# Moving the large SBUF tiles of a transformer layer by 32 bytes, on to multiples of 64 bytes

## The chip, the core and the metric

One core of a Trainium2 chip runs the whole layer as one program. The metric is device time in microseconds, the median of three runs. On this core TensorE (PE in the profile) multiplies, VectorE (DVE) and ScalarE (ACT) do the elementwise work, GpSimd (POOL) takes a few powers and sums, and the transfers are issued from SyncE (SP). SBUF, the memory on the core, has 128 partitions; a tile is a run of bytes at the same place of each partition, and "where a tile lies" below is that place, its address in the partition in bytes.

## What is computed

The layer has 512 rows of 1024 floats. Its parts, with the norms left out:

```
x = x + 0.5 * (silu(h @ wg) * (h @ wu)) @ wd          # ffn1, h = rmsnorm(x), hidden width 2816
h = rmsnorm(x)
o_a, o_b, o_c = three attentions on h @ w_in          # o_c attends to 256 memory rows
y = sum_i sigmoid(h @ w_gate_i + b_i) * (o_i @ w_branch_i)
x = x + y @ w_out
x = x + 0.5 * (silu(h @ wg) * (h @ wu)) @ wd          # ffn2
```

All of it is in float32.

## The kernel before

**Three matmuls for one.** A float32 operand is kept as a pair, hi and lo, of the faster type fp32r: `split` (lines 75 to 78) rounds it to hi on ACT (L77) and takes the difference lo on DVE (L78). A product then is three matmuls: hi by hi, hi by lo and lo by hi. In the profile's names of a matmul the first name behind the arrow is the **moving** operand, whose columns stream through the array, and the second is the **stationary** one, which a weight load (PEld) puts into the array before. Every matmul of the kernel has its own weight load, of 128 columns.

**The feed-forward layers.** `ffn` runs twice. The up product (`mm7`, L354) has as stationary operand a block of weights, 128 of whose columns are loaded at a time, and as moving operand 256 columns of M, the combined activations (`mhi`, `mlo`). Weight blocks go round a ring of six: four lie in the pool `base` (`whi`, `wlo`), two in the layer's own pool (`fhi`, `flo`). A job is 24 such matmuls to one PSUM bank. The down product (`mm3`, L110 to L112) has as stationary operand the gated hidden activations (`gh`, `gl`) and as moving operand 512 columns of a weight block, which again is `whi`/`wlo` or `fhi`/`flo` by turns of the same ring. So the same two kinds of weight tiles are met by M in the up product and by G in the down product.

**The mixing part.** Projections have 384 moving columns of a weight block (`whi`) against `hh`, `hl`, the rows of h, as stationary operand. Gates have 512 moving columns of `hh`, `hl` against weights `fh`, `fl`; branches have 512 moving columns of an attention's output (`och`, `oah`, `obh` and their lo halves) against `fh`, `fl`. The output product has a weight block against `yh`, `yl`. The order on TensorE in this part is written out by hand in the `PLAN_` strings; in the feed-forward layers `run_jobs` sets it.

**Where tiles lie.** Pools on the left side are stacked from the bottom of a partition up, those on the right side from the top down, and each tile takes a multiple of 32 bytes. `base` is first on the left and stays for the whole program; in it `mhalf` (L263, 32 bytes) comes after the identities, and later `le`, another small one. `hb` (96 bytes) lies in the pool `mix`. M and then h lie on the right side. In the built program of before this gives, as the remainder of the tile's address by 64 and by 128 (the offsets at which matmuls read inside them are all multiples of 128 bytes):

| tiles | before, by 64 | before, by 128 | changed, by 64 | changed, by 128 |
|---|---|---|---|---|
| `mhi`, `mlo` (M) | 32 | 96 | 0 | 64 |
| `whi`, `wlo` (base) | 32 | 32 | 0 | 64 |
| `fhi`, `flo` (ffn pool) | 0 | 64 | 0 | 0 |
| `gh`, `gl` (G) | 0 | 64 | 0 | 0 |
| `hh`, `hl` (h) | 32 | 96 | 0 | 64 |
| `fh`, `fl` (gate and branch weights) | 32 | 32 | 0 | 0 |
| `och`, `oah`, `obh`, `yh` and lo halves | 0 | 64 | 0 | 0 |
| `qk` | 0 | 64 | 0 | 0 |
| `kx` | 32 | 32 | 0 | 64 |
| `mkh`, `mkl` / `cqh`, `cql` | 32 / 32 | 32 / 32 | 0 / 0 | 64 / 0 |
| `wraw` (landing of weights) | 0 | 0 | 0 | 0 |

Of the kernel before, what the change touches and what calls it, by code (L numbers as in the profile page):

```python
# [11 lines left out]
F32 = mybir.dt.float32  # L12
# [6 lines left out]
P = 128  # L19
# [20 lines left out]

CHUNKS = (4, 6, 6, 6)
HS = S // 2
LAMBDA_INIT = 0.8 - 0.6 * math.exp(-0.3 * 0)
C_SCALE = 128 ** -0.5

# [2 lines left out]
def layer_kernel(ctx: ExitStack, tc: tile.TileContext, a: dict, out: bass.AP):  # L48
    nc = tc.nc

    base = ctx.enter_context(tc.tile_pool(name="base", bufs=1))
# [23 lines left out]
    def split(raw, hi, lo, engine=None):  # L75

        nc.scalar.copy(out=hi, in_=raw)  # L77
        (engine or nc.vector).tensor_tensor(out=lo, in0=raw, in1=f32(hi), op=ALU.subtract)  # L78
# [84 lines left out]
    def right_pool(name):  # L163
        return tc.tile_pool(name=name, bufs=1, side="right", reuse_waits="tile")
# [6 lines left out]
    def new_M(pool):  # L171
        mh, ml = (pool.tile([P, 7, 4, HS], F32R, name=n) for n in ("mhi", "mlo"))
        return {i: (mh[:, i - 1], ml[:, i - 1]) for i in range(1, 8)}
# [11 lines left out]
    class Operands:  # L185
# [19 lines left out]
        def combine(self, t):  # L205
# [17 lines left out]
            if t == 3:  # L223
                lo, hi = slice(0, HS), slice(HS, S)
                split(t1, *M[5])
# [7 lines left out]
    def squares(src):  # L233
# [4 lines left out]
            square_half(src[:, d], dump[:, d], ss[:, dh:dh + 1])  # L238
        return ss

    Mp = right_pool("M1")
    M1 = new_M(Mp.__enter__())
    memp = tc.tile_pool(name="memp", bufs=1, reuse_waits="tile")
# [15 lines left out]
    make_identity(nc, ident)  # L259
    identr = base.tile([P, P], F32R, name="identr")  # L260
    nc.vector.tensor_copy(out=identr, in_=ident)
    mhalf = base.tile([P, 8], F32, name="mhalf")
    nc.vector.memset(mhalf, -0.5)  # L263

    warm = bank("s")
# [66 lines left out]
    def ffn(pre, x_sb, M, fp, after, raws=None, before_last=None, after_half=None):  # L332
# [12 lines left out]
        def mm7(ps, blk, m, first):  # L345

            for j in range(2):
                c = slice(j * HS, (j + 1) * HS)
                for k in range(4):
# [7 lines left out]
        class Item:  # L357
# [47 lines left out]
            def gated(self, c, f, th):  # L405

                if self.pr[f] is None:
                    self.pr[f] = fp.tile([P, S], F32, tag="pr", name="pr", bufs=3)
                    self.n = 0
                sg = fp.tile([P, HS], F32, tag="sg", name="sg", bufs=2)  # L410
                nc.scalar.activation(out=sg, in_=c[:, :HS], func=AF.Silu)
                pr, cols = self.pr[f], slice(th * HS, (th + 1) * HS)
                nc.vector.tensor_tensor(out=pr[:, cols], in0=sg, in1=c[:, HS:], op=ALU.mult)
# [196 lines left out]
    for t in range(NT):  # L610
# [5 lines left out]
    nc.sync.dma_start(out=la, in_=a["a_lambda"].rearrange("(u v) d -> u v d", u=2).partition_broadcast(P))  # L616
    lp = heads(lam[:, 256:384], 2)
    nc.vector.tensor_tensor(out=lp, in0=la[:, :, 0, :], in1=la[:, :, 1, :], op=ALU.mult)
    le = base.tile([P, 4], F32, name="le")
    nc.vector.tensor_reduce(out=le[:, 0:2], in_=lp, axis=AX.X, op=ALU.add)  # L620
    nc.scalar.activation(out=le[:, 0:2], in_=le[:, 0:2], func=AF.Exp)
    nlam = le[:, 2:3]

    nc.vector.tensor_scalar(out=nlam, in0=le[:, 1:2], scalar1=-LAMBDA_INIT, scalar2=le[:, 0:1],
                            op0=ALU.add, op1=ALU.subtract)
# [13 lines left out]
    mp = mix.__enter__()  # L639


    def bcast(name, src, n):
        g = mp.tile([P, n], F32, name=name)
        nc.sync.dma_start(out=g, in_=src.partition_broadcast(P))
        return g

    gsub = bcast("gsub", a["a_sub_norm"], 128)
    nc.vector.tensor_scalar(out=gsub, in0=gsub, scalar1=1.0 - LAMBDA_INIT, scalar2=None, op0=ALU.mult)
    gb = mp.tile([P, 2, 64], F32, name="gb")
# [16 lines left out]
            nc.gpsimd.tensor_tensor(out=sg[:, :, c, o], in0=sg[:, :, c, o],  # L666
                                    in1=ga[:, c, i].unsqueeze(1).broadcast_to([P, NT, 32]), op=ALU.mult)

    hb = mp.tile([P, 24], F32, name="hb")
    with nc.allow_non_contiguous_dma(reason="3072 words, once"):  # L670
        nc.sync.dma_start(out=hb, in_=a["b_gate"].rearrange("(n p) -> p n", p=P))
    nc.vector.tensor_scalar(out=hb, in0=hb, scalar1=0.5, scalar2=None, op0=ALU.mult)
# [455 lines left out]
```

## Time and profile before

| | |
|---|---|
| median of three runs | 1274.46 us (1273.98 to 1274.72) |
| the profiled execution's own time | 1273.05 us |
| its span, first to last instruction | 1271.3 us |
| mean granted TensorE clock | 0.987 of full speed |
| PE busy / DVE busy / ACT busy | 97% / 66% / 47% of the span |

The span is what the trace shows; 1.75 us of the execution's time lie around it. A matmul's duration in the profile includes its way through the array, so matmuls that follow each other overlap, and the busy share of PE says that it always had one under way, not that it was at its peak. The distance from the start of a matmul to the start of the next is what counts for time.

### The profile page before, as it was taken

How to read it: one execution, taken by the hardware profiler on the slowest of the kernel's cores; microseconds unless marked ns; L12 is line 12 of the kernel's file. 1: busy time of each engine (PE TensorE's matmuls, PEld its weight loads, DVE VectorE, ACT ScalarE, POOL GpSimd, SP SyncE). 2: the span in 40 equal slices, each digit the busy share in tenths (PEclk: the TensorE clock that was granted, in tenths of full speed). 3: DMA queues.
4: the chain of work that ended last, by engine and by line, in shares of the span. 5: the costliest groups of instructions: out<-in, count | busy, mean ns of one | idle time of the engine just before them, and what ended most of it. 6: DMA issues, size and time to landing. Idle time of an engine off the chain costs nothing.

```text
span 1271.3 us, 19657 instructions
## 1 busy us (share of the span) xinstructions
PE 1232.4 (97%) x7808; PEld 1116.9 (88%) x7808; DVE 842.8 (66%) x1377; ACT 596.8 (47%) x1115; POOL 107.1 (8%) x108
## 2 busy tenths in 40 slices
PE   7799999999998999999999999999979999999997
PEld 7789989989986799999999999888878998998996
DVE  7977667667564756766765565453697766766753
ACT  7535425435443446554555454443463452543543
POOL 1100000000000301111221121020000000000002
PEclk8899999999999899999999999999989999999999
DMA  5533324322334403321222320254133242342311
GB/s 215 174 108 116 115 71 128 113 91 101 116 118 130 109 28 108 88 67 58 88 87 70 89 83 31 75 159 160 34 127 122 76 133 91 101 129 73 130 35 67
DMA packets 53084, 127.57 MB, mean 100 GB/s; under 512 B 10112, under 2 KB 10624, under 8 KB 52992
## 3 DMA queue, kind: packets, MB, share of 16 engines
q1 hardware_dynamic: 52416, 125.27, 30.9%
q8 instruction: 61, 1.00, 0.3%
q10 hardware_dynamic: 576, 1.05, 0.2%
q14 instruction: 31, 0.25, 0.1%
HBM read 122.11 MB, written 4.19 MB: 99 GB/s over the span
## 4 chain that ended last, share of the span: by engine, by line
PE 90%; DVE 4%; DMA 2%; ACT 1%; POOL 1%; issue 1%; SPq 0%; POOLq 0%; ACTq 0%; DVEq 0%
PE ps_s L354 19%; PE ps_g L110 9%; PE ps_g L112 9%; PE ps_g L111 9%; PE ps_o L354 5%; PE ps_p L110 4%; PE ps_p L354 4%; PE ps_p L111 4%; PE ps_p L112 4%; PE ps_g L354 4%; PE ps_s L110 2%; PE ps_s L112 2%; PE ps_s L111 2%; PE ps_o L881 2%; PE ps_s L849 2%; PE ps_t L697 1%
## 5 line engine op out<-in xcount | busy, mean ns | idle before, releaser
L77 ACT CAST whi<-wraw 128x1024 fp32r<-128x1024 f32 (+1 forms) x120 | 119.0, 993 | 141.3 <-PE ps_s L354 68.6
L78 DVE TENSOR_TENSOR wlo<-wraw,whi 128x1024 fp32r<-128x1024 f32 (+1 forms) x120 | 137.9, 1151 | 65.6 <-ACT whi L77 64.6
L354 PE MATMUL ps_s<-mhi,whi 128*128 128x256 f32 x496 | 138.3, 279 | 2.3 <-ACT snap L397 2.0
L354 PE MATMUL ps_s<-mlo,whi 128*128 128x256 f32 x496 | 137.7, 278 | 0.0
L354 PE MATMUL ps_s<-mhi,wlo 128*128 128x256 f32 x496 | 136.8, 278 | 0.0
L77 ACT CAST whi<-quarter 128x1024 fp32r<-128x1024 f32 x54 | 56.7, 1051 | 91.8 <-PE ps_s L354 22.7
L354 PEld LDWEIGHTS ps_s<-mhi,whi 128*128 128x128 f32 x496 | 93.8, 189 | 4.1 <-ACT snap L397 2.8
L110 PE MATMUL ps_p<-whi,hh 128*128 128x384 f32 (+1 forms) x264 | 94.8, 359 | 0.0
L354 PEld LDWEIGHTS ps_s<-mlo,whi 128*128 128x128 f32 x496 | 93.7, 189 | 1.0 <-DVE mlo L78 0.2
L354 PEld LDWEIGHTS ps_s<-mhi,wlo 128*128 128x128 f32 x496 | 93.2, 189 | 0.0
L112 PE MATMUL ps_p<-whi,hl 128*128 128x384 f32 (+1 forms) x264 | 89.2, 338 | 0.0
L111 PE MATMUL ps_p<-wlo,hh 128*128 128x384 f32 (+1 forms) x264 | 89.2, 338 | 0.0
L78 DVE TENSOR_TENSOR wlo<-quarter,whi 128x1024 fp32r<-128x1024 f32 x54 | 65.9, 1221 | 24.5 <-ACT whi L77 24.5
L110 PE MATMUL ps_g<-hh,fh 128*128 128x512 f32 x192 | 78.4, 408 | 0.0
L112 PE MATMUL ps_g<-hh,fl 128*128 128x512 f32 x192 | 75.8, 395 | 0.0
L111 PE MATMUL ps_g<-hl,fh 128*128 128x512 f32 x192 | 75.7, 394 | 0.0
L834 DVE CAST kx<-ps_t 128x256 fp32r<-128x256 f32 x32 | 13.6, 425 | 83.7 <-PE ps_t L832 83.7
L121 POOL TENSOR_TENSOR rsh<-msh,mhalf 128x4 f32<-128x4 f32 x38 | 45.2, 1191 | 276.9 <-DVE msh L127 225.2
L78 DVE TENSOR_TENSOR fl<-wraw,fh 128x768 fp32r<-128x768 f32 x48 | 50.0, 1042 | 26.1 <-ACT fh L77 26.1
L77 ACT CAST fhi<-quarter 128x1024 fp32r<-128x1024 f32 x34 | 35.5, 1049 | 59.1 <-PE ps_s L354 16.4
L354 PE MATMUL ps_s<-mhi,fhi 128*128 128x256 f32 x208 | 59.2, 285 | 2.5 <-ACT fhi L77 2.5
L354 PE MATMUL ps_s<-mlo,fhi 128*128 128x256 f32 x208 | 58.9, 283 | 0.0
(376 smaller groups left out, 3662.8 us busy)
## 6 DMA issues: line engine op xcount, KB each, us to landing
wraw<-in_ffn_w SPq DMA_DIRECT2D x88, 512.0 KB, 4.0
wraw<-in_ffn_wd SPq DMA_DIRECT2D x44, 512.0 KB, 3.9
wraw<-in_w_u SPq DMA_DIRECT2D x32, 384.0 KB, 3.3
wraw<-in_w_gb SPq DMA_DIRECT2D x32, 384.0 KB, 3.0
wraw<-in_w_gf SPq DMA_DIRECT2D x16, 384.0 KB, 3.1
wraw<-in_w_mem_kv SPq DMA_DIRECT2D x8, 512.0 KB, 4.1
wraw<-in_w_out SPq DMA_DIRECT2D x8, 512.0 KB, 4.5
x_sb<-in_x SPq DMA_DIRECT2D x4, 512.0 KB, 7.0
```

The costliest lines, as they stand in the source:

```text
L77: nc.scalar.copy(out=hi, in_=raw)
L78: (engine or nc.vector).tensor_tensor(out=lo, in0=raw, in1=f32(hi), op=ALU.subtract)
L110: nc.tensor.matmul(ps, lhsT=st[0], rhs=mv[0], start=first, stop=False)
L111: nc.tensor.matmul(ps, lhsT=st[0], rhs=mv[1], start=False, stop=False)
L112: return nc.tensor.matmul(ps, lhsT=st[1], rhs=mv[0], start=False, stop=last)
L121: nc.gpsimd.tensor_tensor(out=rs, in0=ms, in1=mhalf[:, :n], op=ALU.pow)
L354: nc.tensor.matmul(ps[:, c], lhsT=x, rhs=y, start=first and j + k + n == 0, stop=k == 3 and n == 2, skip_group_check=True)
L697: nc.tensor.transpose(ps[:, j * P:(j + 1) * P], pt[:, j * P:(j + 1) * P], ident)
L834: nc.vector.tensor_copy(out=un.kx[:, :, qs], in_=heads(p2[:, 0:256], 2))
L849: nc.tensor.matmul(out_, lhsT=q, rhs=k, start=j == 0, stop=j == 1)
L881: nc.tensor.matmul(o[:, vs], lhsT=pT[:, j * P:(j + 1) * P], rhs=un.v[:, j, vs], start=j == 0, stop=j == i)
```

## The change

Three small tiles are widened so that what lies behind them in their pool moves, and a pool of one 32-byte tile, which nothing reads or writes, is opened at the outer end of the right side before M.

```
+LINE = 16
...
+    linep = ctx.enter_context(tc.tile_pool(name="line", bufs=1, side="right"))
+    linep.tile([P, 8], F32, name="line")
     Mp = right_pool("M1")
...
-    mhalf = base.tile([P, 8], F32, name="mhalf")
+    mhalf = base.tile([P, LINE], F32, name="mhalf")
     nc.vector.memset(mhalf, -0.5)
...
-    le = base.tile([P, 4], F32, name="le")
+    le = base.tile([P, LINE], F32, name="le")
...
-    hb = mp.tile([P, 24], F32, name="hb")
+    hb = mp.tile([P, 2 * LINE], F32, name="hb")[:, :24]
```

On the left side, tiles behind `mhalf` move up by 32 bytes, those behind `le` by 64, those behind `hb` in its pool by 96; on the right side everything moves down by 32. Every large tile then lies on a multiple of 64 bytes (the table above). The instructions of all five engines and the transfers stand in the same order as before, with the same shapes and tiles; the one difference is that the memset of `mhalf`, once at the start on DVE, writes 128x16 elements instead of 128x8.

## Rows read from the trace of the kernel before

**Rows 1.** The page's part 1: busy us, share of the span, instructions.
```profile
PE 1232.4 (97%) x7808; PEld 1116.9 (88%) x7808; DVE 842.8 (66%) x1377; ACT 596.8 (47%) x1115; POOL 107.1 (8%) x108
```

**Rows 2.** Windows: each stretch's length, then busy us per engine, clock, DMA.
```profile
core 0: us, PE busy (x) PEld busy (x) DVE busy (x) ACT busy (x) POOL busy (x), PEclk, DMA share, GB/s
0.00:100.00 100.00, 84.50 (x545) 76.48 (x546) 82.07 (x102) 55.10 (x88) 11.01 (x12) 0.91 0.48 164
100.00:380.00 280.00, 280.00 (x1962) 259.64 (x1961) 193.52 (x234) 125.57 (x183) 2.20 (x4) 1.00 0.33 107
...
480.00:840.00 360.00, 359.76 (x2094) 325.46 (x2093) 221.82 (x581) 181.74 (x471) 63.97 (x60) 1.00 0.26 78
...
915.00:1000.00 85.00, 75.90 (x529) 70.22 (x528) 72.92 (x83) 41.98 (x56) 0.00 (x1) 0.96 0.34 112
1000.00:1200.00 200.00, 200.00 (x1443) 187.46 (x1442) 141.08 (x162) 87.83 (x121) 0.00 (x0) 1.00 0.31 99
```

**Rows 3.** Timeline of PE, first and last of a run: start us, duration us.
```profile
140.23 0.28 PE L354 MATMUL ps_s<-mhi,fhi 128*128 128x256 f32 x1
...
142.63 0.28 PE L354 MATMUL ps_s<-mhi,flo 128*128 128x256 f32 x1
142.75 0.28 PE L354 MATMUL ps_o<-mhi,whi 128*128 128x256 f32 x1
...
145.36 0.28 PE L354 MATMUL ps_o<-mhi,wlo 128*128 128x256 f32 x1
```

**Rows 4.** Groups by form, up product: count, busy us, mean ns, idle before.
```profile
L354 PE MATMUL ps_s<-mlo,whi 128*128 128x256 f32 x496 | 137.7, 278 | 0.0
...
L354 PE MATMUL ps_s<-mlo,fhi 128*128 128x256 f32 x208 | 58.9, 283 | 0.0
...
L354 PE MATMUL ps_p<-mlo,whi 128*128 128x256 f32 x96 | 26.6, 277 | 0.0
...
L354 PE MATMUL ps_p<-mlo,fhi 128*128 128x256 f32 x64 | 18.1, 283 | 0.0
```

**Rows 5.** The same view, down product of the feed-forward layers.
```profile
L111 PE MATMUL ps_g<-wlo,gh 128*128 128x512 f32 x120 | 47.5, 396 | 0.0
...
L110 PE MATMUL ps_g<-fhi,gh 128*128 128x512 f32 x56 | 22.1, 395 | 1.6 <-ACT gh L77 1.6
L111 PE MATMUL ps_g<-flo,gh 128*128 128x512 f32 x56 | 21.9, 390 | 0.0
...
L111 PE MATMUL ps_p<-wlo,gh 128*128 128x512 f32 x24 | 9.5, 396 | 0.0
```

**Rows 6.** The same view, mixing part: gates, projections, branches; output product (tile view: min/median/max).
```profile
L111 PE MATMUL ps_p<-wlo,hh 128*128 128x384 f32 x256 | 86.0, 336 | 0.0
...
L111 PE MATMUL ps_g<-hl,fh 128*128 128x512 f32 x192 | 75.7, 394 | 0.0
...
L112 PE MATMUL ps_g<-och,fl 128*128 128x512 f32 x32 | 12.7, 396 | 0.0
...
L111 PE MATMUL ps_s<-wlo,yh x16: 392/396/398, 846.7 to 910.8; 128*128 128x512 f32 x16
```

**Rows 7.** Groups by form, short scores of the mixing part.
```profile
L849 PE MATMUL ps_s<-kx,qk 128*128 128x256 f32 x32 | 8.3, 281 | 0.0
L849 PE MATMUL ps_s<-qk 128*128 128x256 f32 x32 | 8.3, 281 | 0.0
...
L111 PE MATMUL ps_g<-mkl,cqh 128*128 128x256 f32 x16 | 4.5, 281 | 0.0
```

**Rows 8.** Groups by form, split on ACT and on DVE.
```profile
L77 ACT CAST whi<-wraw 128x1024 fp32r<-128x1024 f32 x88 | 92.2, 1049 | 127.5 <-PE ps_s L354 68.6 <-PE ps_g L112 21.9 <-issue 12.6
...
L77 ACT CAST fhi<-wraw 128x1024 fp32r<-128x1024 f32 x30 | 31.5, 1050 | 39.8 <-PE ps_s L354 27.9 <-PE ps_p L354 3.8 <-PE ps_o L354 3.1
...
L78 DVE TENSOR_TENSOR wlo<-wraw,whi 128x1024 fp32r<-128x1024 f32 x88 | 107.4, 1222 | 54.7 <-ACT whi L77 54.4
...
L78 DVE TENSOR_TENSOR flo<-wraw,fhi 128x1024 fp32r<-128x1024 f32 x30 | 36.7, 1223 | 20.5 <-ACT fhi L77 19.9
```

## Prediction

> **What bounds the kernel now.** I read the page's busy times first: PE has a matmul under way for 97% of the span, DVE is busy 66%, ACT 47% [rows 1]. That alone is an average, so the windows come next [rows 2]. In the feed-forward stretches from 100 to 380 and from 1000 to 1200 us PE is busy all the time, DVE 193.52 of 280 and 141.08 of 200 us (69% and 71%): nothing that feeds PE is late there, and every nanosecond between two matmul starts is a nanosecond of the program. The mixing stretch from 480 to 840 us is as full (359.76 of 360). Only the first 100 us and the start of the second feed-forward layer are otherwise: PE 84.50 of 100 and 75.90 of 85 us, with DVE at 82% and 86% of its time, so there PE at times waits for DVE's splits. The change adds no work and moves no instruction; what it can change is how far apart matmuls start, so the rest is about that.
>
> **What stands in the trace about the places of tiles.** In one run of the up product, 20 steps from 140.23 to 142.63 us with `fhi`/`flo` as weights are 0.1200 us each; right behind it 23 steps from 142.75 to 145.36 us with `whi`/`wlo` are 0.1135 us each [rows 3]. M, the bank's size, the columns and the order are the same; the weight tile is another one. The grouped durations differ by the same amount, 283 against 277 or 278 ns [rows 4], so from here on a difference of durations is read as a difference of distances.
>
> Taken alone that could say that the ffn pool is a bad place for a weight. The down product says no: there `flo` takes 390 ns and `wlo` 396 [rows 5]; the tile that was slow is now the quick one, and the other way round. What the four cases have in common is the pair. `whi` and M both lie 32 bytes past a multiple of 64, `fhi` and G both on one; these pairs are quick, and the two mixed pairs are slow by about 6 ns, for 256 columns as for 512. A cost per matmul that doesn't grow with the columns fits the weight load, which has 128 columns in either case and runs while the matmul before it streams. So my reading is: a matmul costs some 6 ns more when its moving tile and its stationary tile differ in their place by half of 64 bytes. After the change no pair does.
>
> The Trainium skill speaks against this reading: "TensorE: Matmul & The Clock Gate", Part 2, on the LDWEIGHTS step, says that PE reads weights and the moving operand over two independent SBUF ports, so that the load takes nothing from the running matmul. By that rule the places of the two could not matter to each other, the sum would be zero and the time 1274.5 us; the rows on the crossed pairs do not agree with it.
>
> **The change part by part.** The sum is made against the profiled execution, 1273.05 us (span 1271.3), which is 1.4 us under the median of 1274.46.
>
> 1. *Up product with `fhi`/`flo`.* Against M in bank `ps_s` there are 208 of each of the three kinds, in `ps_p` 64 [rows 4], and 64 each in two more groups of the same sort (`ps_o`, `ps_g`): 400 x 3 = 1,200 matmuls. At 0.1200 - 0.1135 = 6.5 ns each, 7.8 us. The two stretches where PE waits for DVE hold 545 + 529 matmuls [rows 2]; if a quarter of these is of this sort, as in the feed-forward layers as a whole (1,200 of 4,752: these, 2,496 up with `whi`, 720 and 336 down), it is 270, of which I count half. That leaves 1,065 x 6.5 = 6.9 us. Bounds: 5 us (if the two stretches give nothing and the step is 5.5 ns) and 7.8.
> 2. *Down product with `whi`/`wlo`.* Groups of 120 and 24 are shown, with 60 and 36 more in `ps_s` and `ps_o` [rows 5]: 240 x 3 = 720 matmuls of 396 ns. The quick pair has 390; but an `fhi` group whose matmuls often begin a run has 395, so I take 4.2 ns, 3.0 us. Bounds 1.5 (2 ns) and 4.3 (6 ns).
> 3. *Output product*, a weight block against `yh`/`yl`: 32 of each of six kinds, 192 matmuls at 396 [rows 6]. Same pair of places as in 2, 4.5 ns: 0.9 us, bounds 0.3 and 1.2.
> 4. *Branches* (288 matmuls, nine groups like the `och` row at 396) and the memory products (96, `mwh` against `mh`). Both are mixed pairs. But the gates beside them are a matched pair and take 394 [rows 6], not 390, so in this part matched pairs are no more than 2 to 3 ns quicker: 384 x 2.6 = 1.0 us, bounds 0 and 2.3 (6 ns).
> 5. *Gates and projections.* These 576 and 768 matmuls are matched before and after (both tiles 32 past, then both on a line): 0. I can't exclude that both on a line is better than both 32 past: gates would go from 394 to the 390 of the quick down product, and projections, at 336, by the same 4 ns; 1,344 x 4 = 5.4 us is the upper bound.
> 6. *Elementwise work and transfers.* The split of a `wraw` tile into `whi`, 32 past, takes 1049 ns on ACT, into `fhi`, on a line, 1050; on DVE 1222 and 1223 [rows 8]. So nothing is to be had or lost on these engines, and `wraw`, where weights land, keeps its remainder. DVE at 71% still covers PE when PE is 1% quicker. The eight more columns of the one memset and the wider `le` and `hb`, whose used parts are unchanged, cost nothing that the rows could show: the memset runs once, before the first weights are split.
>
> Sum: 6.9 + 3.0 + 0.9 + 1.0 = 11.8 us. From 1273.05 that is 1261.25; on the scale of the median 1262.7, and I say 1262.5. The bounds added up, 6.8 and 21.0 us, give 1267.7 and 1253.5.
>
> **The rivals.**
>
> *The pair's place does not matter, no change.* For it: the short score matmuls of the mixing part. With 256 columns, `qk` against `qk`, both on a line, takes 281 ns and `kx` against `qk`, a mixed pair, 281 too [rows 7]. Whatever makes `fhi` slow against M would then be something else that the change leaves, such as how far apart the two tiles are. Against it: these are runs of four matmuls, each begun by other work, while the 6 ns are seen in unbroken runs of 24, over more than a thousand matmuls. Time 1274.5 us. "SBUF — State Buffer", Specifications, in the Trainium skill puts SBUF's cacheline at 16 bytes; by that every tile here was on a line already, and this rival is what would follow, but no row shows a line's size.
>
> *The quick pair of the up product becomes slow: slower.* `whi` and M are quick while both lie 32 past and 64 apart by 128 (32 and 96 in the table of places). After the change both are at 64 by 128, at the same place. There is no long run of 256 columns with such a pair in the trace; the nearest are the short ones at the same place by 128, `qk` with itself and `mkl` against `cqh`, both 281 [rows 7], 4 ns over the 277 of now. There are (496 + 128 + 112 + 96) x 3 = 2,496 of these matmuls (the first and the last of these four groups are shown [rows 4]). At 4 ns they cost 10.0 us; 1 would give only 2 ns (283 to 281) or 2.4 us, 3 and 4 at most 1.9 and 2 1.5: together 5.8, so 4.2 us slower, 1278.7. At 6 ns it would be 15.0 against 5.8: 1283.7. It decides from 11.8 / 2,496 = 4.7 ns on, if all else goes as I count it. Against it: `fhi` against G is at the same place by 128 (64 and 64) and is the quickest pair of 512 columns, 390 [rows 5].
>
> *More than I count.* If gates, projections and branches, too, come down to the level of the quick pairs (the upper bounds of 4 and 5), 17 to 21 us go: 1254 to 1257. For it: the quickest 512 columns have both tiles on a line. Against it: the mixing part differs in its short runs as well.
>
> **How the numbers follow.** The forecast with its own range, 1253.5 to 1267.7, has 0.73, the larger gain included (0.13 of it); no change 0.14; slower by the second rival 0.13. Of the forecast everything is faster by over 0.2% (under 1271.9), which is about the least that a measurement of this kernel can tell from no change. From no change I move 0.02 to faster, since half effects lie between, and from the second rival 0.01 to no change: 0.75, 0.13 and 0.12. The range from 1253 to 1275 holds the forecast and most of the no-change case and leaves out the slower one and a little at the lower end.
>
> **What would show it.** If I am right: up-product groups with `fhi` at 277 to 278 like those with `whi`, runs of 24 matmuls of 2.73 us where they were 2.88; down-product groups with `wlo` at 390 to 392; `whi` against M unchanged at 277; ACT and DVE splits unchanged to a few ns; the gates within 4 ns of 394. The second rival shows at once as 281 or more in the `whi` groups of L354. If the groups move and the time doesn't, PE waits that are now hidden, on ACT's `whi` or DVE's `wlo`, must have grown in the full stretches, and PE's 100% there would be gone. What would make the prediction wrong is above all that the pair's remainder by 64 is not the cause but only goes with it in this one layout: there are four long cases, and all four agree with it, but also with rules that the changed layout would not satisfy.

## The result and the profile after

The changed kernel takes 1284.13 us (1283.15 to 1284.66, four runs) beside 1274.22 us (1272.85 to 1274.72, four runs) for the kernel before on the same chip: ratio 1.0079 [1.0061, 1.0096]. It is slower by 9.9 us, where 11.8 us less was forecast. The profiled execution took 1284.04 us (span 1282.2), 11.0 us over that of before.

The page's part 1 of the changed kernel, to be read against [rows 1]: PE alone has more to do, 10.8 us more, with the same number of instructions.

```profile
PE 1243.2 (97%) x7808; PEld 1126.6 (88%) x7808; DVE 843.8 (66%) x1377; ACT 597.3 (47%) x1115; POOL 107.4 (8%) x108
```

The windows of the changed kernel, with the columns of [rows 2]:

```profile
core 0: us, PE busy (x) PEld busy (x) DVE busy (x) ACT busy (x) POOL busy (x), PEclk, DMA share, GB/s
100.00:380.00 280.00, 280.00 (x1945) 260.16 (x1944) 190.40 (x228) 123.93 (x181) 1.64 (x3) 1.00 0.32 102
...
1005.00:1205.00 200.00, 200.00 (x1416) 187.27 (x1415) 136.99 (x157) 86.21 (x117) 0.00 (x0) 1.00 0.31 98
```

PE is still never without a matmul in the feed-forward stretches and its clock is full, but it starts 1945 where it started 1962 in the same 280 us, and 1416 for 1443 in 200 us (a stretch set 5 us later). The average matmul has become a little dearer, and no wait was added: the span less PE's busy time is 38.9 us before (1271.3 less 1232.4) and 39.0 after (1282.2 less 1243.2). The groups by form say which; here the up product:

```profile
L359 PE MATMUL ps_s<-mlo,whi 128*128 128x256 f32 x496 | 140.1, 283 | 0.0
...
L359 PE MATMUL ps_s<-mlo,fhi 128*128 128x256 f32 x208 | 58.3, 280 | 0.0
...
L359 PE MATMUL ps_p<-mlo,whi 128*128 128x256 f32 x96 | 27.0, 282 | 0.0
...
L359 PE MATMUL ps_p<-mlo,fhi 128*128 128x256 f32 x64 | 17.9, 280 | 0.0
```

Against [rows 4] the quick tile `whi` went from 278 and 277 to 283 and 282, and the slow one, `fhi`, only from 283 to 280. The timeline shows the same in the run that [rows 3] showed: 24 matmuls with `whi`, whose 23 steps now take 2.73 us (0.1187 us each, 0.1135 before).

```profile
144.14 0.28 PE L359 MATMUL ps_o<-mhi,whi 128*128 128x256 f32 x1
...
146.87 0.28 PE L359 MATMUL ps_o<-mhi,wlo 128*128 128x256 f32 x1
```

The other products, in the order of [rows 5] and [rows 6]: down product 396 to 394 with `wlo` and 390 to 391 with `flo`, projections 336 to 338, gates 394 to 395, branches 396 to 395.

```profile
L113 PE MATMUL ps_p<-wlo,hh 128*128 128x384 f32 x256 | 86.4, 338 | 0.0
...
L113 PE MATMUL ps_g<-hl,fh 128*128 128x512 f32 x192 | 75.8, 395 | 0.0
...
L113 PE MATMUL ps_g<-wlo,gh 128*128 128x512 f32 x120 | 47.3, 394 | 0.0
...
L113 PE MATMUL ps_g<-flo,gh 128*128 128x512 f32 x56 | 21.9, 391 | 0.0
...
L114 PE MATMUL ps_g<-och,fl 128*128 128x512 f32 x32 | 12.6, 395 | 0.0
```

The splits did not move, as [rows 8] stands now:

```profile
L80 DVE TENSOR_TENSOR wlo<-wraw,whi 128x1024 fp32r<-128x1024 f32 x88 | 107.5, 1222 | 59.1 <-ACT whi L79 59.0
...
L79 ACT CAST whi<-wraw 128x1024 fp32r<-128x1024 f32 x88 | 92.2, 1049 | 136.4 <-PE ps_s L359 72.4 <-PE ps_g L114 21.9 <-issue 13.3
```

**Where the time went.** One window over the whole run, of the up product's line alone (the columns are length, PE and PEld busy, clock, DMA share, GB/s), first in the kernel before, then in the changed one:

```profile
0.00:1290.00 1290.00, 441.40 (x3696) 437.18 (x3696) 0.99 0.31 99
```

```profile
0.00:1290.00 1290.00, 451.05 (x3696) 446.70 (x3696) 0.99 0.31 99
```

The 3,696 matmuls of the up product keep PE busy for 9.65 us more, nearly all of the loss. Worked out from the trace's start times, as the mean from the start of one matmul to the start of the next of the same product at the full clock, `whi` against M went from 114.2 to 119.1 ns and `fhi` against M from 120.3 to 118.2: 2,496 x 4.9 = 12.2 us lost, 1,200 x 2.1 = 2.5 us gained. By the same means projections lost 2.0 to 2.3 ns (768 of them, 1.5 to 1.8 us), gates 1.4 to 1.9 (576, 0.8 to 1.1 us), branches gained 1.1 to 1.3 (288, 0.3 to 0.4 us), and down and output products stayed within some 0.4 ns; the spread is that of which steps across a pause are left out.

### The profile page after: what moved, and what is told of

It is laid out like the page before. It is cut to its first block, busy times and chain, and to the rows that moved or that the text cites. A ratio compares the mean times of both kernels' runs of the same rounds, so it can differ in the third digit from the quotient of the medians.

```text
span 1282.2 us, 19657 instructions
## 1 busy us (share of the span) xinstructions
PE 1243.2 (97%) x7808; PEld 1126.6 (88%) x7808; DVE 843.8 (66%) x1377; ACT 597.3 (47%) x1115; POOL 107.4 (8%) x108
## 4 chain that ended last, share of the span: by engine, by line
PE 91%; DVE 4%; ACT 1%; DMA 1%; issue 1%; POOL 1%; SPq 0%; POOLq 0%; ACTq 0%; DVEq 0%
PE ps_s L359 19%; PE ps_g L112 9%; PE ps_g L114 9%; PE ps_g L113 9%; PE ps_o L359 5%; PE ps_p L359 4%; PE ps_p L112 4%; PE ps_p L113 4%; PE ps_p L114 4%; PE ps_g L359 4%; PE ps_s L112 2%; PE ps_s L114 2%; PE ps_s L113 2%; PE ps_o L886 2%; PE ps_s L854 2%; PE ps_t L702 1%
## 5 line engine op out<-in xcount | busy, mean ns | idle before, releaser
L79 ACT CAST whi<-wraw 128x1024 fp32r<-128x1024 f32 (+1 forms) x120 | 119.1, 993 | 150.5 <-PE ps_s L359 72.4
L359 PE MATMUL ps_s<-mhi,whi 128*128 128x256 f32 x496 | 140.9, 285 | 2.3 <-ACT snap L402 2.0
L123 POOL TENSOR_TENSOR rsh<-msh,mhalf 128x4 f32<-128x4 f32 x38 | 45.3, 1193 | 278.9 <-DVE msh L129 233.7
```

The source lines that it names most:

```text
L123: nc.gpsimd.tensor_tensor(out=rs, in0=ms, in1=mhalf[:, :n], op=ALU.pow)
L359: nc.tensor.matmul(ps[:, c], lhsT=x, rhs=y, start=first and j + k + n == 0, stop=k == 3 and n == 2, skip_group_check=True)
```

## The experiments

Two measures are used below. The times in words are medians, with the ratio to the kernel before on the same chip and its 95% interval. **Distance** is the place of the stationary tile minus that of the moving tile, as a remainder by 256 bytes; the remainders by 64 and 128 that stand ahead of the prediction do not give it. In the built programs it is:

| product (columns), moving and stationary tile | before | changed |
|---|---|---|
| up (256), M and `whi` | 64 | 128 |
| up (256), M and `fhi` | 96 | 192 |
| down (512), `whi` and G | 32 | 64 |
| down (512), `fhi` and G | 0 | 0 |
| projections (384), `whi` and h | 192 | 128 |
| gates (512), h and `fh` | 192 | 64 |
| branches (512), `och` and its like and `fh` | 96 | 128 |

The texts set down before each run number their theories: 1, both places count, each by itself; 2, only the distance counts; 3, the place is not the cause; 4, what ran before counts as well; 5, 64 apart and both 32 past a multiple of 64 is what is quick. They call the runs by short names, which stand in parentheses behind the titles below.

**1. All pairs of places, matmuls alone** (pairs). The layer is left out. Eight moving tiles `mA` to `mH` and eight stationary ones `wA` to `wH` lie, as remainders by 256, in steps of 32 bytes (H is 224 past A), and PE runs all 64 pairs with 256 columns and again with 512, with nothing else at work, in one execution.

```
+ for cols, n in ((256, 16), (512, 8)):
+     for i in range(8):
+         for j in range(8):
+             run(mv[i], st[j], cols, n)
```

> This kernel leaves out the layer: it copies x to the output and runs nothing but matmuls, 48 in a row for each of 64 pairs of a moving and a stationary tile, first with 256, then with 512 columns. The tiles A to H lie 0, 32, ... 224 bytes past a multiple of 128 (A and E on one). Theory 1 (both places by 128 count, not only their difference): with 256 columns mD against wB (96 and 32, as M and whi before) is 276 to 278 ns, mC against wC (64 and 64, as now) and mC against wA (64 and 0) 280 to 284, mD against wC 283; and the table repeats after four tiles. Theory 2 (only the distance of the two counts, by 256): the table is the same along its diagonals. Theory 3 (the place is not it; what other engines do at the time is): all 64 pairs within 1 ns of each other.

Some of the 128 groups, count, busy us, mean ns, idle before. With 512 columns D with D (distance 0) takes 389, D with B (192) 391, D with C (224) 395; with 256 columns A with D (distance 96) takes 280, D with G (96 as well) 283:

```profile
L46 PE MATMUL ps<-mD,wG 128*128 128x256 f32 x48 | 5.9, 283 | 0.0
...
L46 PE MATMUL ps<-mA,wA 128*128 128x256 f32 x48 | 5.9, 283 | 0.0
...
L46 PE MATMUL ps<-mA,wC 128*128 128x256 f32 x48 | 5.8, 281 | 0.0
...
L46 PE MATMUL ps<-mA,wD 128*128 128x256 f32 x48 | 5.8, 280 | 0.0
...
L46 PE MATMUL ps<-mD,wB 128*128 128x512 f32 x24 | 5.7, 391 | 0.0
...
L46 PE MATMUL ps<-mD,wC 128*128 128x512 f32 x24 | 5.8, 395 | 0.0
...
L46 PE MATMUL ps<-mD,wD 128*128 128x512 f32 x24 | 5.6, 389 | 0.0
```

Worked out from the start times (ns from start to start, the first ten of a group left out, mean over the eight pairs of a distance, or both values where they fall into two; the row of 384 columns is from experiment 2):

| distance | 0 | 32 | 64 | 96 | 128 | 160 | 192 | 224 |
|---|---|---|---|---|---|---|---|---|
| 512 columns | 226.7 | 233.5 | 233.5 | 234.5 | 233.6 | 233.7 | 228.8 | 233.2 |
| 256 columns | 120.0 | 118.4 | 113.3 or 117.8 | 117.3 or 120.0 | 118.7 | 120.0 | 117.8 | 116.7 or 117.8 |
| 384 columns | 173.3 | 173.4 | 174.8 | 173.4 | 175.6 | 176.9 | 173.4 | 176.5 |

So the place of a pair does count with nothing else at work, by up to 7.8 ns, and what counts is the distance. A match by 64 is a distance of 0, 64, 128 or 192; these are not alike, and the quickest is another one for 512 columns (0) than for 256 (64). With 256 columns some distances have two values. At 64 two of eight pairs, D with F and H with B, ran at 113.3, the others at 117.8. At 96 two of eight, D with G and H with C, ran at 120.0, the others at 117.3; these two are the ones that stand right behind the two quick pairs. Whether the order matters needed another run.

**2. The pairs in another order** (pairs_turned). The same kernel, stationary tile outside, moving tiles turned, 384 columns instead of 512.

```
- for cols, n in ((256, 16), (512, 8)):
-     for i in range(8):
-         for j in range(8):
-             run(mv[i], st[j], cols, n)
+ for cols, n in ((256, 16), (384, 8)):
+     for j in range(8):
+         for i in range(8):
+             run(mv[(3 * i + j) % 8], st[j], cols, n)
```

> Leaves out the layer as the kernel of pairs did: matmuls alone, the same 64 pairs of places, with 256 and this time 384 columns, in another order of the pairs, so that each pair follows another one. If a pair's places alone decide (theory 1), 256 columns give the same table as before: 113.4 ns from start to start for mD against wF and mH against wB alone, 117 to 120 elsewhere. If what ran before a run decides too (theory 4), the quick cells move among the four pairs that are 96 and 32 by 128 (mD and mH against wB and wF), and one of the two that were slow becomes quick. 384 columns: mF against wD (32 and 224 by 256, as whi and h before) 173 to 174, mG against wC or its like (64 and 192) 175 to 177.

Groups of this run; the first is the pair that took 281 in experiment 1.

```profile
L46 PE MATMUL ps<-mA,wC 128*128 128x256 f32 x48 | 5.6, 277 | 0.0
...
L46 PE MATMUL ps<-mD,wF 128*128 128x256 f32 x48 | 5.6, 277 | 0.0
```

All eight pairs at distance 64, each behind a pair at 160, now ran at 113.3 ns. Every other distance repeated a value of experiment 1 within 0.2 ns; all eight pairs at 96 ran at 117.3 and all eight at 224 at 116.6. The distance of 64 has two rhythms with 256 columns, and the same two tiles can be in either.

**3. Half of the change: the right side only** (right_only). M and h move by 32 bytes, the left side stays.

```
+    linep = ctx.enter_context(tc.tile_pool(name="line", bufs=1, side="right"))
+    linep.tile([P, 8], F32, name="line")
```

> Only the 32 bytes on the right side. M goes to 64 by 128, whi stays at 32, fhi and G at 64. Theories 1 and 2: whi against M becomes a pair that differs by 32 and goes from 277 to 283 ns (2,496 x 6 = 15 us), fhi against M comes to the same place and goes to 280 to 282 (-2 us), the down product stays: 1286 to 1289 us. Theory 3 (not the place of these pairs): 1274 us within 2.

**4. The other half: the three widened tiles only** (left_only).

```
-    mhalf = base.tile([P, 8], F32, name="mhalf")
+    mhalf = base.tile([P, 16], F32, name="mhalf")
...
-    le = base.tile([P, 4], F32, name="le")
+    le = base.tile([P, 16], F32, name="le")
...
-    hb = mp.tile([P, 24], F32, name="hb")
+    hb = mp.tile([P, 32], F32, name="hb")[:, :24]
```

> Only the three widened tiles. M stays at 96 by 128, whi goes to 64, fhi and G to 0. Theories 1 and 2: both weight tiles differ from M by 32, so whi goes from 277 to 283 ns (15 us) and fhi stays at 283; down product with whi as in the changed kernel, 394 to 395 (-1 us): 1286 to 1290 us. Theory 3: 1274 within 2, or 1284 if the left side alone is the cause.

They took 1285.15 us, 1.0096 [1.0081, 1.0111], and 1284.68 us, 1.0091 [1.0076, 1.0106], each about 1 us under the range of theories 1 and 2. Groups of the up product, right side only, then left side only:

```profile
L356 PE MATMUL ps_s<-mlo,whi 128*128 128x256 f32 x496 | 139.6, 282 | 0.0
...
L356 PE MATMUL ps_s<-mlo,fhi 128*128 128x256 f32 x208 | 58.8, 283 | 0.0
```

```profile
L354 PE MATMUL ps_s<-mlo,whi 128*128 128x256 f32 x496 | 139.4, 282 | 0.0
...
L354 PE MATMUL ps_s<-mlo,fhi 128*128 128x256 f32 x208 | 58.7, 282 | 0.0
```

Either half alone costs as much as the whole. Each moves `whi` away from M's distance of 64 (to 96), which is what they have in common with the whole change (128).

**5. The layer's own pool moved by 96 bytes** (ffn_32). The line stands in both feed-forward layers. `fhi` and G move together, so that `fhi` comes to a distance of 192 from M.

```
+    fp.tile([P, 24], F32, name="fpad")
```

> The kernel before, with 96 bytes at the start of both feed-forward pools, so that fhi, flo and G lie at 32 by 128, where whi lies, 32 past a line; all large tiles of these layers are then 32 past. Theory 1: fhi against M is the pair 96 and 32 and goes from 283 to 277 or 278 ns (1,200 x 6 = 7 us); the down product (32 against 32) is not known, 390 to 396: 1263 to 1269 us. Theory 2 (distance by 256, 64 here as for fhi in the changed kernel): fhi at 280, 1269 to 1272 us.

1267.72 us, 0.9956 [0.9939, 0.9973]. The `fhi` group fell by 6 ns, the size that term 1 of the prediction hoped for, while `whi` kept its 278. The time lies in the range of theory 1, whose rule experiment 1 puts out; theory 2, which reckoned with one value for a distance (280 for `fhi`), missed it:

```profile
L354 PE MATMUL ps_s<-mlo,whi 128*128 128x256 f32 x496 | 137.8, 278 | 0.0
...
L354 PE MATMUL ps_s<-mlo,fhi 128*128 128x256 f32 x208 | 57.7, 277 | 0.0
```

**6. M moved by 64, the base tiles by 64** (swap_64). `whi` comes to a distance of 192, `fhi` to 224.

```
+    linep.tile([P, 16], F32, name="line")
...
+    mhalf = base.tile([P, 24], F32, name="mhalf")
```

> The kernel before with everything on the right side 64 bytes lower and everything behind mhalf 64 higher: M at 32 by 128 and whi at 96, fhi and G at 0. The pair of the up product is as before 64 apart and both 32 past a multiple of 64, but with the two places exchanged. If both 32 past and 64 apart is what makes it quick (theory 5), whi stays at 277 and the time is within 3 us of 1274. If the places themselves count, 96 for the moving tile and 32 for the stationary one (theory 1), whi goes to 281 to 283 as in the changed kernel and the time to 1282 to 1288.

1283.13 us, 1.0081 [1.0064, 1.0098]. Theory 5 is out. At 192, where `fhi` was quick in experiment 5, `whi` takes 280 here (the table behind experiment 12 shows it as a case of the slow rhythm):

```profile
L356 PE MATMUL ps_s<-mlo,whi 128*128 128x256 f32 x496 | 138.8, 280 | 0.0
```

**7. Both weight tiles at the best distances of the tables** (ffn_best): 64 from M in the up product, 0 from G in the down product. The line again stands in both layers.

```
+    fp.tile([P, 56], F32, name="fpad")
```

> The kernel before with 224 bytes at the start of both feed-forward pools: fhi, flo and G then lie at 32 by 256, as whi does, M stays at 224. Theory 1 with the tables of pairs: up product with fhi 277 (from 283, 1,200 x 6 = 7 us); down product with whi at the same place as G by 256, 390 (from 396, 720 x 6 = 4 us): 1262 to 1264 us. If for 512 columns the distance by 256 does not count in this kernel, as ffn_32: 1267 to 1268.

1274.68 us, 1.0011 [1.0002, 1.0021], over 10 us above the 1262 to 1264 that were expected. The down product came to 389 as expected, and the up product, its distances 64 as in the kernel before, fell to the slow rhythm:

```profile
L354 PE MATMUL ps_s<-mlo,whi 128*128 128x256 f32 x496 | 140.2, 283 | 0.0
...
L354 PE MATMUL ps_s<-mlo,fhi 128*128 128x256 f32 x208 | 58.5, 281 | 0.0
...
L111 PE MATMUL ps_g<-wlo,gh 128*128 128x512 f32 x120 | 46.7, 389 | 0.0
```

**8. The mixing part too** (all_best). As 7, and `fh` and the attentions' outputs moved to the place of h.

```
+    mo.tile([P, 40], F32, name="mopad")
...
+    hb = mp.tile([P, 64], F32, name="hb")[:, :24]
```

> As ffn_best, with 160 bytes at the start of the pool mixo and hb at 256 bytes, so that fh, fl, h and the attention outputs all lie at 224 by 256: gates and branches (864 matmuls of 512 columns) get tiles at the same place by 256. Theory 1: gates from 394 to 390 or 391, branches from 396 to 390 or 391, the output product (32 and 224) 392: 3 to 5 us below ffn_best, 1258 to 1260. If in this part the short runs decide, as the matched pairs there did not show any gain: within 1 us of ffn_best.

1271.99 us, 0.9991 [0.9982, 1.0000]: 2.7 us under experiment 7, where 3 to 5 were expected. Gates came from 394 to 391, branches (`och`) from 396 to 394.

**9. What runs before** (pairs_order). The layer is left out again. Pairs at distance 64 and at 192, 96 matmuls each, follow another pair whose distance is varied.

```
+ for apart in (2, 6):
+     for i in range(8):
+         n = i if i != apart else 8
+         run(pm[i], pw[(i + n) % 8], 256 if n < 8 else 512, 16 if n < 8 else 8)
+         run(mv[i], st[(i + apart) % 8], 256, 32)
```

> Matmuls alone, without the layer. Runs of 96 with 256 columns whose stationary tile lies 64 bytes (first eight) or 192 bytes (last eight) behind the moving one by 256, each right after a run of another distance on other tiles: 0, 32, (512 columns at 0), 96, 128, 160, 192, 224 bytes for the first eight, 0, 32, 64, 96, 128, 160, (512 columns at 0), 224 for the last. Theory 4 (a distance of 64 has a quick and a slow rhythm, and what ran before decides which): some of the first eight at 276 to 277 ns, some at 280 to 281, and slow after 512 columns at 0. If the distance alone decides (theory 2): all eight the same, 276 to 277. The last eight, theory 4: mostly 280 to 281, quick after the run at 64 if that one was quick.

```profile
L46 PE MATMUL ps<-mC,wE 128*128 128x256 f32 x96 | 11.5, 281 | 0.0
L46 PE MATMUL ps<-mB,wD 128*128 128x256 f32 x96 | 11.5, 281 | 0.0
...
L46 PE MATMUL ps<-mF,wH 128*128 128x256 f32 x96 | 11.5, 281 | 0.0
...
L46 PE MATMUL ps<-mG,wE 128*128 128x256 f32 x96 | 11.5, 279 | 0.0
L46 PE MATMUL ps<-mD,wF 128*128 128x256 f32 x96 | 11.1, 276 | 0.0
...
L46 PE MATMUL ps<-mC,wA 128*128 128x256 f32 x96 | 11.0, 276 | 0.0
```

At distance 64 the run is quick (276) after a pair at 96 (`mD,wF`), 128 or 192, and slow (281) after 0, 32 (`mB,wD`), 160 (`mF,wH`), 224 or 512 columns at 0 (`mC,wE`). At distance 192 it is quick after 0, 64 (`mC,wA`) or 96, and slow (279) after 32, 128, 160, 224 or 512 columns at 0 (`mG,wE`). A group's mean stands for all 96 matmuls: a run stays in the rhythm it fell into. Each of these cases was run once, and the distance of the pair before does not settle the rhythm by itself: behind 160 a distance of 64 is slow here and was quick in eight of eight pairs in experiment 2, and behind 32 it was quick in two of seven in experiment 1.

**10. All large tiles on multiples of 64, other distances** (lines_apart). The changed kernel with the same four small tiles, widened otherwise; up distances 64 (`whi`) and 192 (`fhi`).

```
-    linep.tile([P, 8], F32, name="line")
+    linep.tile([P, 56], F32, name="line")
...
-    le = base.tile([P, LINE], F32, name="le")
+    le = base.tile([P, 32], F32, name="le")
...
-    hb = mp.tile([P, 2 * LINE], F32, name="hb")[:, :24]
+    hb = mp.tile([P, 64], F32, name="hb")[:, :24]
```

> The changed kernel with every large tile still on a multiple of 64, but at other ones: M and h at 0 by 256, whi at 64, fhi and G at 192, fh and attention outputs at 192. The distances by 256 from the moving to the stationary tile of the feed-forward layers are then those of ffn_32 (64, 192, 128 and 0). Theories 2 and 4 (distance by 256): up product 276 to 278 ns with both kinds of weights, 1265 to 1270 us. Theory 1, or that tiles on lines of 64 are bad for the up product in themselves: 280 to 283, 1280 to 1286 us.

1267.09 us, 0.9943 [0.9926, 0.9959]: 17.0 us under the changed kernel, with every remainder by 64 the same as there. The up product alone gives most of it: the window over the whole run has 436.00 us for its line, against 451.05. The distances of the mixing part moved too (projections and gates back to 192, branches to 0).

```profile
L359 PE MATMUL ps_s<-mlo,whi 128*128 128x256 f32 x496 | 138.0, 279 | 0.0
...
L359 PE MATMUL ps_s<-mlo,fhi 128*128 128x256 f32 x208 | 57.8, 278 | 0.0
```

```profile
0.00:1290.00 1290.00, 436.00 (x3696) 431.88 (x3696) 0.99 0.31 99
```

**11. Quick rhythm and quick down product** (ffn_mix). The second line stands in both layers. From the kernel before: up distances 64 and 192; down 0 for `whi`, 128 for `fhi`.

```
+            fp.tile([P, 32], F32, tag="gpad", name="gpad")
...
+    fp.tile([P, 56], F32, name="fpad")
```

> The kernel before with G at 32 by 256 (as whi) and fhi, flo at 160: up product 64 and 192 apart, as ffn_32, down product with whi 0 apart, with fhi 128 apart. Theory 4, with the change between the two kinds of weights bringing the up product back to the quick rhythm: up 277 to 278, down 390 with whi and 396 with fhi, 1264 to 1267 us. If the down product at distance 0 leaves the up product in the slow rhythm, as in ffn_best: up 280 to 281, 1275 to 1278 us.

1265.43 us, 0.9934 [0.9920, 0.9949], within the 1264 to 1267 of theory 4.

**12. The same with the mixing part of experiment 8** (mix_both).

> ffn_mix with the two pads of all_best (fh, h and the attention outputs at 224 by 256). If what the two gave adds up, as it does where the distance of each pair sets its own matmuls' time: 1265.4 less the 2.7 us by which all_best was under ffn_best, 1262 to 1264 us, gates at 392 and branches at 391 to 392 ns. If it does not add up: 1265 to 1266.

1263.19 us (1262.35 to 1263.74, five rounds) beside 1273.99: 0.9913 [0.9899, 0.9926], the quickest of all, faster than both kernels. Its groups, and the page's part 1:

```profile
L354 PE MATMUL ps_s<-mlo,whi 128*128 128x256 f32 x496 | 138.1, 279 | 0.0
...
L111 PE MATMUL ps_g<-hl,fh 128*128 128x512 f32 x192 | 75.1, 391 | 0.0
...
L354 PE MATMUL ps_s<-mlo,fhi 128*128 128x256 f32 x208 | 57.7, 277 | 0.0
...
L111 PE MATMUL ps_g<-wlo,gh 128*128 128x512 f32 x120 | 46.8, 390 | 0.0
```

```profile
PE 1221.0 (97%) x7808; PEld 1109.8 (88%) x7808; DVE 842.8 (67%) x1377; ACT 596.5 (47%) x1115; POOL 106.9 (8%) x108
```

**The rhythms inside the layer.** With experiment 9 the up products of all these kernels can be read stretch by stretch. The table is worked out from the start times: stretches of at least 20 up matmuls with one sort of weight tile that follow a stretch with the other sort, at full clock; quick are those whose median step, from the fifth matmul on, is under 116 ns. In parentheses are the distances of the stretch and of the one before it.

| kernel | `whi` after `fhi`: quick | `fhi` after `whi`: quick |
|---|---|---|
| before | 47 of 48 (64 after 96) | 0 of 31 (96 after 64) |
| changed | 0 of 48 (128 after 192) | 0 of 31 (192 after 128) |
| 5, layer's pool by 96 | 47 of 48 (64 after 192) | 25 of 31 (192 after 64) |
| 6, M and base by 64 | 2 of 47 (192 after 224) | 0 of 30 (224 after 192) |
| 7, best of the tables | 4 of 47 (64 after 64) | 3 of 30 (64 after 64) |
| 10, multiples of 64 | 45 of 48 (64 after 192) | 23 of 31 (192 after 64) |
| 12, quickest | 47 of 48 (64 after 192) | 28 of 30 (192 after 64) |

Where experiment 9 has the case (64 after 96 or 192 quick; 192 after 64 quick, after 128 or 224 slow), most stretches of the layer agree with it, 23 of 31 where the fewest do. In the changed kernel `fhi` stands at a distance that can be quick and is slow in every stretch; `whi` before it is at 128, and 192 after 128 was slow in experiment 9 too. Kernel 7 has one distance throughout. There all 16 `whi` stretches right behind a down product are slow, and most of those that follow stay so.

## Why the prediction was wrong

**What held.** PE was the bound and stayed it: 100% busy in the same feed-forward stretches, and its busy time and the span grew alike (10.8 and 10.9 us). That a pair's places cost some nanoseconds per matmul is shown by experiment 1, where PE works alone; so the rival by which the pair's place doesn't matter is out. The rule of independent ports ("TensorE: Matmul & The Clock Gate", Part 2, LDWEIGHTS, in the Trainium skill), by which, as the prediction drew from it, the places of weights and moving operand could not matter to each other, does not agree with these runs: 226.7 against 233.5 ns for the same 512 columns. Term 6 (ACT, DVE, transfers: 0) held to a nanosecond.

**The step that failed** is the rule taken from four cases: "a matmul costs some 6 ns more when its moving tile and its stationary tile differ in their place by half of 64 bytes. After the change no pair does." The durations it rested on were right, the thing they have in common was not. The two quick pairs [rows 4, 5] were quick each at its own distance: `whi` and M at 64, the quickest for 256 columns; `fhi` and G at 0, the quickest for 512. With 256 columns a distance of 0 takes 120.0 ns, with 512 one of 64 takes 233.5, so neither is quick for both; 192 comes nearest to that, with 228.8 for 512 and, in the quick rhythm of experiment 9, 113.3 for 256. The two slow pairs are cases of distance too: `whi` and G at 32, and `fhi` and M at 96, which takes 120.0 in experiment 1 right behind a quick run at 64, as it stands in the layer. Matching by 64 only leaves distances of 0, 64, 128 and 192; the change put `whi` at 128 from M, and experiment 10, which keeps the match and changes the distances, is 17.0 us quicker. The prediction itself named this as what would make it wrong: that the remainder "only goes with it in this one layout".

**The terms.** Term 1 (-6.9 us) came to about -2.5: `fhi` at 192 ran at 118.2 ns, in the slow rhythm of that distance, behind a distance of 128; experiment 5 has the same distance at 277 ns after 64, so a gain of the forecast size was there to be had. Term 2 (-3.0) and term 3 (-0.9) came to nothing from start to start: down products moved from 32 to 64, which are 233.5 alike alone. Term 4 (-1.0) came to about -0.3. Term 5 was 0 and came to 2.3 to 2.9 us lost. And "`whi` against M unchanged at 277" missed 12.2 us, more than all the gains forecast.

**The second rival** is what happened: `whi` against M slow, at 283 where 281 or more was its mark, and 1284.13 where its upper case gave 1283.7. Its price of 4 to 6 ns was 4.9, on the 2,496 matmuls it counted. That the time met its upper case is partly luck: at 4.9 ns its own sum, 12.2 us less the 5.8 of gains that it kept, gives 1280.9, but those gains, with what term 5 lost, came to about nothing. It had 0.13 because `fhi` against G, the same place by 128, was the quickest pair; that argument carried a 512-column row over to 256 columns, and experiment 1 shows the two lengths have different quick places.

**What stays open.** Why the spacing depends on the distance at all, and what begins the quick rhythm or the slow one. The distance of what ran just before does not settle it, as experiments 1, 2 and 9 show between them, and the layer too: `whi` at 64 behind a down product of `fhi` at distance 0 is quick in 4 of 4 stretches of the kernel before and in 0 of 4 of kernel 7, and experiment 9 has 64 slow behind 512 columns at 0. So the rhythm of a new layout is not to be foretold from its distances alone. Two parts of the change were tried as halves; the three widened tiles were not tried singly. `fhi` at 96 took 120.3 ns in the layer; alone 96 takes 117.3, 120.0 or, in one run of experiment 9, 118.7, and which of these follows from what is shown only for 120.0 (behind a quick run at 64, in two of two pairs of experiment 1 and in all 28 stretches of the kernel before that follow a `whi` stretch seen to be quick; three more follow one too short to tell). In kernel 12 gates and branches, at distance 0, step at about 230 ns, and alone that distance takes 226.7; that is not explained. Places finer than 32 bytes were not tried.

## What to carry to other kernels

Where TensorE is busy all the time with short matmuls that each load their own weights, compare the groups of one shape that differ only in their tiles: a difference of 5 ns on thousands of matmuls is a per cent, and padding of some bytes in a pool moves it either way (1263.19 to 1285.15 us here, the same instructions in the same order). Don't take a rule for placement from the few pairs that one layout has: run the pairs alone, for the column count in question, and then in the kernel, since what ran before counts too. What made one product quick (a distance of 0 for 512 columns) was slow for the next one (120.0 ns for 256, and no distance was slower).

## What the runs showed of the hardware

The start-to-start time of fp32r matmuls with a weight load each depends on the distance of the two tiles by 256 bytes: 226.7 to 234.5 ns for 512 columns, 173.3 to 176.9 for 384, 113.3 to 120.0 for 256. With 384 and 512 columns pairs of equal distance were alike, wherever they lie, within about 1 ns. With 256 columns it depends on what ran before as well. At distances of 64 and 192 a run settles in one of two rhythms, 276 to 277 or 279 to 281 ns in duration, and keeps it for all of 96 matmuls: 113.3 or 117.8 ns from start to start alone, 113 or 118 in the layer. A distance of 96 was met at 117.3, 118.7 and 120.0 ns.
